# Summing the first head's projection over K-tiles while its modulation is still being loaded, in a two-layer diffusion block

## The chip, the cores and the metric

The kernel runs on one core of a Trainium2 chip. The metric is the device time of one launch in microseconds. The core has five engines that work side by side and meet through semaphores: PE (TensorE, matrix products), DVE (VectorE), ACT (ScalarE), POOL (GpSimd) and SP (SyncE, which here issues most of the DMAs). PEld is the loading of PE's stationary operand.

## What is computed

A latent stream `x` (512 tokens by 1024) and a context stream `ctx` (256 tokens by 1024) pass through two layers; only the latent stream is returned. Each layer is a mixer and a SwiGLU network, each of them behind a norm that is modulated by a conditioning vector:

```
mx = silu(c) @ mod_w[l] + mod_b[l]        # 6 parts of 1024: shift, scale, gate, twice
mc = silu(c_ctx) @ mod_w[l] + mod_b[l]
hx = rms(x, norm_mix_w[l]) * (1 + scx1) + shx1
hc = rms(ctx, norm_mix_w[l]) * (1 + scc1) + shc1
# layer 0: 16 query heads in 4 groups, one key/value head each
#   groups 0, 1: windowed attention with a sink; groups 2, 3: dense attention
p  = h @ ev_w_in                           # queries, keys, values of all groups
q, k = rope(rms(q)), rope(rms(k))          # context tokens without rope
x  = x + gx1 * (attention @ w_out)
x  = x + gx2 * swiglu(rms(x) * (1 + scx2) + shx2)
# ctx likewise; layer 1 is a differential attention of 8 heads with the same frame
```

All inputs are float32. The kernel keeps that precision in its large products by splitting each operand into a rounded part and a remainder and adding three products: high by high, high by low, low by high.

## The kernel before

The 768 tokens are six tiles of 128: tiles 0 to 3 are `x`, tiles 4 and 5 are `ctx`; `CTX_FIRST` is the order 4, 5, 0, 1, 2, 3. The model width of 1024 is eight K-tiles of 128.

**The start.** SP loads the two context tiles, then the modulation weights of parts 0 and 1 (shift and scale of the first norm) in chunks of 256 columns, with the four tiles of `x` among them. `start_mod(n)` makes both parts' chunk `n` through `mod_chunk`: two pieces of 512 KB are loaded (ring `mw` of six, `start_tile`), 16 small products per piece (eight K-tiles' halves, each in two passes) put both streams' results, spread over four strips of partitions, into a PSUM bank (lines 164 to 172), ACT copies them out as `modr` (174), and PE turns the rows into columns with products against a two-column selector `sel2` (179). `add_mod` adds the bias and, for a scale, forms `aff` (227, 231). Chunk `n` gives shift and scale of the K-tiles `2n` and `2n + 1`.

Beside this each token tile is squared and summed on ACT (843), scaled on DVE (844), transposed on PE (848) and copied by ACT into `xT` (849). When all four chunks are written down, a loop over the K-tiles modulates `xT` in place on DVE (854), rounds it to `hT`/`hTc` on ACT (859) and subtracts for the remainder (860), on DVE for the latent tokens and on POOL for the context.

**The first head group.** `weights0(0, ...)` loads four units of projection weights (three DMAs each, 384 KB), rounds them on ACT (309) and subtracts on DVE (310). `in_proj0` then goes over the six token tiles: `project` adds 24 products of 128 by 384 into one bank (405 to 407), ACT copies the sum to the row buffer `qkv` (451, ring of two), and the rotation follows: squares on ACT (379), sums on DVE (381), reciprocal roots on POOL (148, 149), products with the rope tables on DVE (388, 393 to 396), scaling on POOL (454), the split of queries and keys (456 to 461), transposes of both (468, 474), and copies to `qt` and `kT` (470, 475).

**The later groups.** While the attention of group `b` runs, `in_proj0(b + 1)` is interleaved, one tile after each pair of attention steps, with its sums in the single bank `acc0`, and so are the twelve chunks of modulation parts 2 to 4 (`MODS0`). Four chunks of part 5 follow in the first SwiGLU network.

**Order.** The program is written in one order, and a planner that simulates the engines sets the order of the instructions on each engine; `tc.high_priority(n)` ranks the instructions in its block earlier. On the chip each engine then goes through its own list in that order. PSUM has eight banks: `acc0`, `acc1`, `tr0`, `tr1` and two tiles of two banks each in `p_sc`. The weights' landing room `raw_tile` is a ring of two.

## Time and profile before

| | us |
|---|---|
| median of 3 runs | 1822.0 |
| lowest and highest of them | 1819.93, 1823.89 |
| the profiled execution | 1825.45 |
| its span, first to last instruction | 1823.7 |

A view of windows gives, for each stretch, its length and then busy time and number of instructions of PE, PEld, DVE, ACT and POOL, then the clock granted to PE as a share of full speed, the mean busy share of the 16 DMA engines, and GB/s. A timeline row gives start, duration, engine, line, operation, output and inputs, shape and count, and in brackets the idle time before it with what ended it. A row of grouped instructions gives busy time and mean duration in ns of one, then the idle time in front of them. A matmul's duration is longer than the step from its start to the next one's, since matmuls overlap.

### The profile page before, as it was taken

What the parts mean: (1) busy time and instruction counts of PE and PEld (TensorE: products, weight loads), DVE (VectorE), ACT (ScalarE), POOL (GpSimd) and SP (SyncE); (2) the same over time, 40 slices, a digit from 0 to 9 for tenths busy, and PEclk for the clock granted to TensorE, in tenths of its full rate; (3) what the DMA queues carried; (4) which work ended last, traced back from release to release, by engine and by line L of the source; (5) the groups of instructions that cost most, each with busy time, mean ns of one, the idle gap of its engine ahead of it and who ended that gap; (6) DMA issues with size and microseconds to landing.
All of it is one profiled execution on the core that took longest, in us unless ns stands there. A gap on an engine that the chain in (4) does not pass through costs nothing. (4 is left out here: it accounts for less than half of the span.)

```text
span 1823.7 us, 26198 instructions
## 1 busy us (share of the span) xinstructions
PE 1752.0 (96%) x9958; PEld 1458.2 (80%) x9958; DVE 1002.0 (55%) x1703; ACT 825.5 (45%) x1726; POOL 641.8 (35%) x840
## 2 busy tenths in 40 slices
PE   6999999999999999999999899999998999999998
PEld 4877676667888888888888789999986888888886
DVE  4664545443355555545552657777675455655652
ACT  6555555544354444333331656666664532222220
POOL 2764554632053443222220466666643200000000
PEclk8999999999999999999999899999999999999999
DMA  9111322302543334334330311111103233232221
GB/s 314 46 44 55 96 73 99 131 13 76 180 149 117 103 104 140 115 127 126 117 105 3 102 35 59 44 45 44 42 25 104 90 97 102 82 104 93 93 93 47
DMA packets 152478, 165.65 MB, mean 91 GB/s; under 512 B 16480, under 2 KB 139936, under 8 KB 152352
## 3 DMA queue, kind: packets, MB, share of 16 engines
q1 hardware_dynamic: 152000, 163.77, 28.1%
q8 instruction: 78, 1.28, 0.3%
q14 instruction: 48, 0.39, 0.1%
q10 hardware_dynamic: 352, 0.21, 0.0%
HBM read 159.73 MB, written 4.22 MB: 90 GB/s over the span
## 5 line engine op out<-in xcount | busy, mean ns | idle before, releaser
L750 PE MATMUL pg<-hT,wgh 128*128 128x512 f32 (+1 forms) x736 | 244.8, 386 | 2.2 <-ACT hT L293 2.2
L750 PE MATMUL pu<-hT,wuh 128*128 128x512 f32 (+1 forms) x736 | 244.1, 385 | 0.0
L412 DVE TENSOR_TENSOR dps<-dps,g 128x512 f32<-128x512 f32 x200 | 135.7, 697 | 131.3 <-PE dps L801 126.7
L799 PE MATMUL dps<-wdh,hdh 128*128 128x512 f32 x440 | 176.2, 401 | 5.3 <-DVE x L413 3.5
L800 PE MATMUL dps<-wdl,hdh 128*128 128x512 f32 x440 | 174.0, 396 | 0.0
L801 PE MATMUL dps<-wdh,hdl 128*128 128x512 f32 x440 | 166.4, 396 | 0.0
L750 PEld LDWEIGHTS pg<-hT,wgh 128*128 128x128 f32 x736 | 137.2, 189 | 32.7 <-ACT hT L293 2.4
L750 PEld LDWEIGHTS pu<-hT,wuh 128*128 128x128 f32 x736 | 137.1, 189 | 28.5
L750 PE MATMUL pg<-hT,wgl 128*128 128x512 f32 (+1 forms) x368 | 141.9, 386 | 0.0
L750 PE MATMUL pu<-hT,wul 128*128 128x512 f32 (+1 forms) x368 | 141.5, 384 | 0.0
L413 DVE TENSOR_TENSOR x<-x,dps 128x512 f32<-128x512 f32 x200 | 133.3, 683 | 3.3
L405 PE MATMUL inps<-wih,hT 128*128 128x384 f32 x384 | 133.1, 347 | 0.4 <-ACT qkv L451 0.2
L406 PE MATMUL inps<-wil,hT 128*128 128x384 f32 x384 | 130.6, 340 | 0.0
L407 PE MATMUL inps<-wih,hT 128*128 128x384 f32 x384 | 130.6, 340 | 0.0
L198 ACT ACTIVATE modw<-modw,cols 128x256 f32<-128x256 f32 x192 | 81.9, 498 | 69.4 <-DMA modw<-in_mod_w_dram 66.4
L799 PEld LDWEIGHTS dps<-wdh,hdh 128*128 128x128 f32 x440 | 82.7, 188 | 27.6 <-DVE x L413 4.4
L310 DVE TENSOR_TENSOR wul<-wur,wuh 128x1024 fp32r<-128x1024 f32 x44 | 54.6, 1241 | 89.3 <-ACT wuh L309 89.3
L801 PEld LDWEIGHTS dps<-wdh,hdl 128*128 128x128 f32 x440 | 82.6, 188 | 20.2 <-issue 0.4
L750 PE MATMUL pg<-hTc,wgh 128*128 128x256 f32 x352 | 98.3, 283 | 0.5 <-ACT hTc L293 0.2
L750 PE MATMUL pu<-hTc,wuh 128*128 128x256 f32 x352 | 98.2, 282 | 0.0
L800 PEld LDWEIGHTS dps<-wdl,hdh 128*128 128x128 f32 x440 | 82.8, 188 | 17.6
L777 DVE TENSOR_TENSOR pu<-sg,pu 128x768 f32<-128x768 f32 (+1 forms) x44 | 36.5, 829 | 108.3 <-PE pu L750 94.4
(235 smaller groups left out, 4306.3 us busy)
## 6 DMA issues: line engine op xcount, KB each, us to landing
modw<-in_mod_w_dram SPq DMA_DIRECT2D x96, 512.0 KB, 4.0
wgr<-in_ffn_w_in_dram SPq DMA_DIRECT2D x44, 512.0 KB, 3.4
wur<-in_ffn_w_in_dram SPq DMA_DIRECT2D x44, 512.0 KB, 3.4
wdr<-in_ffn_w_out_dram SPq DMA_DIRECT2D x44, 512.0 KB, 3.5
wir<-in_od_w_in_dram SPq DMA_DIRECT2D x96, 128.0 KB, 2.3
x<-in_x_dram SPq DMA_DIRECT2D x8, 512.0 KB, 3.9
wir<-in_ev_w_in_dram SPq DMA_DIRECT2D x16, 256.0 KB, 2.7
wor<-in_ev_w_out_dram SPq DMA_DIRECT2D x8, 512.0 KB, 4.4
```

The lines of the kernel that those rows point to most:

```text
L198: nc.scalar.activation(pr[:, k], w[:, k], AF.Copy, scale=cols[:, kk:kk + 1])
L310: (sub or nc.vector).tensor_sub(lo, raw, f32(hi))
L405: nc.tensor.matmul(ps, hs[0][:, k, :], a, start=k == 0, stop=False)
L406: nc.tensor.matmul(ps, hs[0][:, k, :], b, start=False, stop=False)
L407: nc.tensor.matmul(ps, hs[1][:, k, :], a, start=False, stop=k == KT - 1)
L412: nc.vector.tensor_mul(tmp, ps, g[:, n * 512:(n + 1) * 512])
L413: eng.tensor_add(xt[:, n * 512:(n + 1) * 512], xt[:, n * 512:(n + 1) * 512], tmp)
L750: nc.tensor.matmul(ps[:, s0:s1], a, cols_T(b, s0, s1)[:, k, :], start=k == 0 and q == 0, stop=k == KT - 1 and q == 2)
L777: nc.vector.tensor_mul(pu, sg, pu)
L799: nc.tensor.matmul(ps, hh, a, start=j == 0, stop=False)
L800: nc.tensor.matmul(ps, hh, b, start=False, stop=False)
L801: nc.tensor.matmul(ps, hl, a, start=False, stop=j == nj - 1)
```

## The change

Four parts.

1. The first group's projection is summed by quarters. Chunk `n` of the modulation (`start_mods`) now makes both parts in one PSUM bank with one copy and one set of transposes, ranked ahead of other work by 400; the products' order, its DMAs and its ring (eight in place of six) are in `start_mods` itself. Behind each chunk stands one unit of projection weights (`unit0`). `start_h(n)` modulates, rounds and splits the two K-tiles of that chunk, alternating ACT and DVE for the modulation. Then `project` adds those two K-tiles to all six token tiles, whose six sums stay open in six banks (`acc0`, `acc1`, and four in `p_sc`). `in_proj0(0)` starts from the finished sums (`banks`).
2. Rows become columns by `mod_cols`, in all chunks that `mod_chunk` makes too: a transpose of each block of 128 and a DVE reduction over the four strips, in place of the products with `sel2`.
3. Of each token tile's two copies into `xT`, the second goes to DVE. The first group's weights are split on POOL and land in `raw_tile`, the second group's are split on DVE.
4. The row buffer `qkv` has four places in place of two (`QBUF`). The mask lands in `raw_tile`. The query tiles `qt` of groups 0 and 2 lie in the pool `even` in place of `wp`.

```diff
+QBUF = 4
...
-    mk = start.pool.tile([P, 2, P], F32, name="mk")
+    mk = raw_tile([P, 2, P], "mk")
...
-        pc2 = p_1.tile([P, nb, 2], F32, name="modcol", tag=bank)
+        add_mod(l, part, k0, k1, mod_cols(r, p_1.tile([P, nb, P], F32, name="modcol", tag=bank)), 2)
+
+    def mod_cols(r, ps):
+
+        nb = ps.shape[1]
         for b in range(nb):
-            nc.tensor.matmul(pc2[:, b, :], r[:, b * P:(b + 1) * P], sel2, start=True, stop=True)
-        add_mod(l, part, k0, k1, pc2, 2)
+            nc.tensor.transpose(ps[:, b, :], r[:, b * P:(b + 1) * P], ident)
+        m = small.tile([P, nb, 2], F32, name="mcol", tag=f"mcol{nb}")
+        nc.vector.tensor_reduce(m, ps.rearrange("p b (j r) -> p b r j", r=32)[:, :, 0:2, :], AX.X, ALU.add)
+        return m
...
-    def project(ps, t, ws, c0, c1):
+    def project(ps, t, ws, c0, c1, ks=range(KT)):
...
-        for k in range(KT):
+        for k in ks:
...
         for t in CTX_FIRST:
-            ps = acc_tile("inps", 384, one=0) if b else p_sc.tile([P, 1024], F32, name="inps", tag="sc")[:, :384]
-            project(ps, t, ws, 0, 384)
-            raw = wp.tile([P, 384], F32, name="qkv", tag="qkv", bufs=2)
+            if banks:
+                ps = banks[t]
+            else:
+                ps = acc_tile("inps", 384, one=0)
+                project(ps, t, ws, 0, 384)
+            raw = wp.tile([P, 384], F32, name="qkv", tag="qkv", bufs=QBUF)
...
-        return start.pool.tile(shape, F32, name=name, tag="mw", bufs=6)
-
-    def start_mod(n):
+        return start.pool.tile(shape, F32, name=name, tag="mw", bufs=8)
+
+    def start_mods(n):
+
+        wm = []
         for part in range(2):
-            mod_chunk(0, part, n, raw_tile if n == 3 and part == 0 else start_tile, start.pool, f"acc{part}", p_sc)
+            c0 = part * D + n * 256
+            for pc in range(2):
+                w = start_tile([P, 4, 256], "modw")
+                nc.sync.dma_start(
+                    w, mod_w[0, pc * 4 * P:(pc + 1) * 4 * P, c0:c0 + 256].rearrange("(j p) n -> p j n", p=P))
+                wm.append(w)
+
+        with tc.high_priority(400):
+            ps = tr_tile("mod", [P, 2, 256])
+            for a, w in enumerate(wm):
+                part, pc = divmod(a, 2)
+                for j in range(4):
+                    nc.tensor.matmul(ps[32 * j:32 * j + 32, part, :], s_pad[:, 4 * pc + j, :], w[:, j, :],
+                                     start=pc == 0, stop=pc == 1, tile_position=(0, 32 * j))
+            r = start.pool.tile([P, 512], F32, name="modr", tag="modr", bufs=1)
+            nc.scalar.copy(r, ps.rearrange("p a n -> p (a n)"))
+            m = mod_cols(r, tr_tile("modcol", [P, 4, P]))
+            for part in range(2):
+                add_mod(0, part, 2 * n, 2 * n + 2, m[:, 2 * part:2 * part + 2], 2)
+
+    def start_h(n, segs):
+
+        ks = slice(2 * n, 2 * n + 2)
+        for s0, s1 in segs:
+            i = s0 // SEQ
+            for k in range(2 * n, 2 * n + 2):
+                z = xT[:, k, s0:s1]
+                sc, sh = aff[0][:, 0, k, i:i + 1], modc[0][:, 0, k, i:i + 1]
+                if k % 2:
+                    nc.scalar.activation(z, z, AF.Identity, bias=sh, scale=sc)
+                else:
+                    nc.vector.tensor_scalar(z, z, sc, sh, ALU.mult, ALU.add)
+            hi, lo = (cols_T(j, s0, s1)[:, ks, :] for j in range(2))
+            nc.scalar.copy(hi, xT[:, ks, s0:s1])
+            (nc.gpsimd if i else nc.vector).tensor_sub(lo, xT[:, ks, s0:s1], f32(hi))
...
-    start_mod(0)
-    start_mod(1)
+    start_mods(0)
+    ws = [unit0(0, 0, wp.pool, nc.gpsimd)]
     xs.update({t: load_x(t) for t in CTX_FIRST[2:]})
...
-            nc.scalar.copy(xT[:, 4 * g:4 * g + 4, t * P:(t + 1) * P], pt)
-    start_mod(2)
-    start_mod(3)
-    for k in range(KT):
...
+            (nc.vector.tensor_copy if g else nc.scalar.copy)(xT[:, 4 * g:4 * g + 4, t * P:(t + 1) * P], pt)
+
+    banks = {t: acc_tile("inps", 384) for t in CTX_FIRST[:2]}
+    for t in (0, 2):
+        two = p_sc.tile([P, 2, 512], F32, name="inps", tag="sc")
+        banks.update({t + a: two[:, a, :384] for a in range(2)})
+    for n in range(4):
+        if n:
+            start_mods(n)
+            ws.append(unit0(0, n, wp.pool, nc.gpsimd))
+        start_h(n, ((SEQ, TOK), (0, SEQ)) if n else ((SEQ, TOK), (0, SEQ // 2), (SEQ // 2, SEQ)))
+        for t in CTX_FIRST:
+            project(banks[t], t, ws, 0, 384, range(2 * n, 2 * n + 2))
...
-    proj = in_proj0(0, ws, tabs, wp.pool, even.pool, wp.pool)
+    proj = in_proj0(0, ws, tabs, wp.pool, even.pool, even.pool, banks)
...
-            ws = weights0(b + 1, wp.pool, nc.gpsimd)
-            proj = in_proj0(b + 1, ws, tabs, wp.pool, (even if b % 2 else odd).pool, (wp if b % 2 else odd).pool)
+            ws = [unit0(b + 1, u, wp.pool, nc.gpsimd if b else nc.vector) for u in range(4)]
+            proj = in_proj0(b + 1, ws, tabs, wp.pool, (even if b % 2 else odd).pool, (even if b % 2 else odd).pool)
```

`unit0(b, u, ...)` is the body of the loop in `weights0`, for one unit.

27 lines of the change are left out of this document (7 added, 20 removed).

## The prediction

> **What bounds the kernel now.** I read the page's busy table first, then its slices, then the windows of the first 85 us and the timeline of TensorE (PE) there, because every edit but one lies in that stretch.
>
> ```profile
> PE 1752.0 (96%) x9958; PEld 1458.2 (80%) x9958; DVE 1002.0 (55%) x1703; ACT 825.5 (45%) x1726; POOL 641.8 (35%) x840
> PE   6999999999999999999999899999998999999998
> DMA  9111322302543334334330311111103233232221
> ```
>
> PE is busy nearly everywhere, the DMA engines only in the first slice of 45.6 us. So the kernel is a DMA-bound head, followed by a PE-bound rest. A microsecond of PE work moved out of the rest into the head is worth up to a microsecond at the end, provided PE then finds other work. The windows show the head in bytes (last column, GB/s), clock (PEclk) and PE time.
>
> ```profile
> 0.00:10.00 10.00, 1.75 (x13) 0.61 (x17) 1.14 (x3) 5.45 (x9) 2.38 (x10) 1.00 0.82 284
> 10.00:20.00 10.00, 9.76 (x65) 5.50 (x57) 1.95 (x5) 5.17 (x10) 0.84 (x3) 1.00 1.06 402
> 20.00:30.00 10.00, 7.04 (x72) 5.10 (x72) 5.72 (x14) 8.53 (x19) 3.66 (x7) 1.00 1.07 376
> 30.00:40.00 10.00, 7.26 (x57) 3.70 (x57) 6.85 (x14) 4.58 (x9) 1.86 (x1) 0.61 1.04 325
> 40.00:50.00 10.00, 10.00 (x45) 10.00 (x46) 9.93 (x18) 4.24 (x8) 7.00 (x2) 0.70 0.27 75
> ```
>
> That is 2.84, 6.86, 10.62 and 13.87 MB in by 10, 20, 30 and 40 us, and then the stream stops. The first projection starts only there:
>
> ```profile
> 40.78 0.67 PE L405 MATMUL inps<-wih,hTc 128*128 128x384 f32 x1
> 41.25 0.52 PE L406 MATMUL inps<-wil,hTc 128*128 128x384 f32 x1
> 41.57 0.52 PE L407 MATMUL inps<-wih,hTc 128*128 128x384 f32 x1
> ...
> 45.80 0.49 PE L405 MATMUL inps<-wih,hTc 128*128 128x384 f32 x1
> 46.13 0.34 PE L406 MATMUL inps<-wil,hTc 128*128 128x384 f32 x1
> 46.30 0.34 PE L407 MATMUL inps<-wih,hTc 128*128 128x384 f32 x1
> ...
> 53.45 0.48 ACT L451 COPY qkv<-inps 128x384 f32<-128x384 f32 x1 [1.90 <-PE inps L407]
> ...
> 72.26 0.33 PE L407 MATMUL inps<-wih,hT 128*128 128x384 f32 x1
> ```
>
> From start to start a projection matmul takes 0.32 us up to 45.8 and 0.173 us after it. The 144 of them (6 tiles, 8 K-tiles, 3 each) run from 40.8 to 72.4; ScalarE (ACT) takes out the first finished sum at 53.45.
>
> **The change: the projection by quarters.** It cuts the 144 matmuls into four groups of 36, each needing only its quarter of the modulation, and holds six sums open in six banks. What a quarter waits for: x (6 tiles, 0.52 MB each), its modulation weights (4 pieces of 0.52 MB) and its projection weights (0.39 MB). These bytes are the same as before, in another order: x now comes behind four pieces of modulation and one of the projection.
>
> ```profile
> 28.01 1.07 ACT L849 COPY xT<-npt 128x512 f32<-128x512 f32 x2
> ...
> 38.05 1.93 PE L171 MATMUL mod<-modw,s_pad 128*32 128x256 f32 x16
> 39.91 1.01 PE L179 MATMUL modcol<-cst,modr 128*128 128x2 f32 x4
> ...
> 42.25 5.17 POOL L860 TENSOR_TENSOR hTc<-xT,hTc 128x512 fp32r<-128x512 f32 x1 [7.81 <-ACT hTc L859]
> ...
> 46.37 1.07 DVE L231 SCALAR_TENSOR_TENSOR aff<-modc,cols 128x4 f32<-128x4 f32 x1
> ...
> 51.58 1.35 DVE L860 TENSOR_TENSOR hT<-xT,hT 128x512 fp32r<-128x512 f32 x1 [0.34 <-ACT hT L859]
> ```
>
> Before, x is all transposed at 29.1 us. With one modulation group less ahead of it (1 MB at 376 to 402 GB/s, some 2.6 us) and half of the evictions moved from ACT to VectorE (DVE), whose windows up to 30 us have room, I estimate 24 us: the first quarter can run over all six tiles from there. The last modulation needs all of x, 16 pieces and three projection units, with 0.4 MB of small inputs 13.1 MB: 10.62 at 30 us and 2.5 more at 325 GB/s give 37.6 us. In the kernel before its scale is done only at 47.4, since the last column matmuls stood behind projection matmuls, and the last operand at 52.9. Ranked first, they follow their weights directly:
>
> ```profile
> 144.59 0.65 PE L553 MATMUL av<-PT,vv 128*64 128x256 f32 x4
> ...
> 145.82 1.07 PE L171 MATMUL mod<-modw,s_pad 128*32 128x256 f32 x16
> 146.83 0.77 PE L543 MATMUL ppt<-cst,Pt 128*128 128x128 f32 x5
> ...
> 148.57 0.56 PE L179 MATMUL modcol<-cst,modr 128*128 128x2 f32 x4
> 148.99 0.64 PE L543 MATMUL ppt<-cst,Pt 128*128 128x128 f32 x4
> 149.56 0.65 PE L553 MATMUL av<-PT,vv 128*64 128x256 f32 x4
> ```
>
> At the full clock 16 modulation matmuls take 1.01 us, four column matmuls 0.42 and four transposes 0.57 from start to start. The last chain is then 1.0 for the last matmuls, some 0.6 for the copy (half of the x2 row above), 0.57 for four transposes, and for the new DVE reduction, which this trace does not show, 0.2 to 0.5 us: between a tiny DVE operation and the 128x320 reduction quoted below. I take 0.3, as it sums only 32 values per partition. With the two small additions and the hand-overs I put it at 3.7 us: 41.3. Modulating, rounding and subtracting a quarter of two K-tiles costs about 4 us more (the x2 row of ACT, 1.07, and the L860 row of DVE, 1.35, are two of three steps), and the context part's subtraction on GpSimd (POOL) ran 5.17 us here, beside a DVE busy 9.93 of 10. So the last quarter's operands are whole at 45 to 47, and by data alone the projection could end at 47 + 24 x 0.173, some 51 us.
>
> PE itself is later. From 24 us it has 132 of the 144 matmuls left (the context tiles' first 12 may go earlier), 22.8 us at 0.173; three modulation groups of 32 matmuls, 6.1 us; their 12 transposes, 1.7. That is 30.6 us: 54.6, and I take **55 us**. The bounds are 50 (data, everything earlier hidden) and 60 (30.6 us begun at 26, with one stretch of 16 matmuls at 0.32, 2.4 us, and a us of waits). Before, the same point is 72.4 less what PE did in between of other work: four tiles' query and key transposes and the last two column groups, together about 2.2 us, so 70.2. **Head start: 15 us** (10 to 20).
>
> **What of it carries.** After 55, PE lives on head 1's projection (25 us) until head 0's rotations have come through. Those are longest on POOL:
>
> ```profile
> L149 POOL TENSOR_TENSOR rs_q<-rs_q,neghalf 128x5 f32<-128x5 f32 x12 | 14.5, 1204 | 0.3
> L454 POOL TENSOR_TENSOR qy<-qy,rs_q 128x320 f32<-128x320 f32 x12 | 8.7, 722 | 0.4
> L381 DVE TENSOR_REDUCE qss<-sq 128x5 f32<-128x320 f32 x12 | 5.8, 479 | 3.5 <-ACT sq L379 3.5
> L461 POOL TENSOR_TENSOR kd<-qy,kd 128x128 fp32r<-128x128 f32 x11 | 5.6, 512 | 2.6 <-ACT es L527 1.7 <-POOL vv L452 0.8
> L452 POOL COPY vv<-qkv 128x64 f32<-128x64 f32 x12 | 4.5, 376 | 2.1 <-ACT qkv L451 2.0
> L148 POOL TENSOR_SCALAR rs_q<-qss 128x5 f32<-128x5 f32 x12 | 3.4, 287 | 8.5 <-DVE qss L381 5.9 <-DVE nm L519 1.8 <-DVE rc L530 0.2
> ```
>
> One tile costs POOL 1.20 + 0.72 + 0.51 + 0.38 + 0.29 = 3.1 us, six 18.6. Six sums now become ready within some 6 us instead of over 19, so this chain turns from hidden to nearly bare: from about 50 to 69, against head 1's projection from 55 to 80. Its cover holds, thinly. Four row buffers instead of two let PE run ahead of the rotation, and head 1's weights can be loaded and split early, since each quarter of head 0's frees its unit. Their subtraction moves from POOL to DVE, four of them, while head 0's moves to POOL, beside the DMA stream, at no cost. I take 4 us of lost PE time (0 to 10). From 110 us on, PE is full again:
>
> ```profile
> 75.00:80.00 5.00, 3.17 (x13) 1.84 (x12) 4.37 (x15) 4.02 (x12) 4.83 (x7) 1.00 0.23 65
> 80.00:85.00 5.00, 4.98 (x24) 4.98 (x25) 2.86 (x14) 3.91 (x14) 3.65 (x9) 0.66 0.29 80
> ...
> 110.00:120.00 10.00, 9.87 (x69) 8.88 (x68) 6.48 (x17) 7.26 (x19) 6.41 (x10) 1.00 0.01 2
> ```
>
> **The columns of later modulations.** Sixteen chunks after the start exchange four column matmuls (0.42 us) for two transposes (0.29): 0.13 us each, 2 us in all on a full PE, with one DVE reduction more in each; the bank is held by one DVE read as before. **The other homes** (mask, query tiles, ring of eight) move no work; I cost them nothing. If an address newly shared makes a wait, it costs about one eviction, 0.5 us per head, and a gain from them is excluded as no transfer starts earlier but those in the head.
>
> **Sum.** 15 - 4 + 2 = **13 us**: the profiled execution's 1825.45 (span 1823.7) becomes 1812.5. That execution is 3.45 above the median of the three runs, 1822.0, which the same saving makes **1809.0**.
>
> **The rivals.** *Rotation-bound (0.18).* If POOL and DVE, not PE, set when head 0's attention can start, only their advance carries: the first sum is ready some 4 to 8 us earlier than its 53.45. With 2 for the columns the gain is about 7: 1815. For it: POOL is busy 4.83 of 5 at 75 to 80, and PE idles there. Against it: those 5 us also carry weight splits that now come earlier, on DVE.
>
> *The stall goes too (0.12).* The 1.83 us of idle PE at 75 to 80 and the low clock after it (0.66, about 1.7 us lost) vanish, nothing is lost, and the data bound is met: 19 + 2 = 21 less, 1801.
>
> *No overlap (0.08).* Engines run in a planned order. If the planner puts the early quarters behind the last modulation, PE waits at its head for the last DMA, and 144 matmuls follow it: what is left is the shorter last chain and the columns, 2 us: 1820.
>
> *Cold quarters (0.12), the slower one.*
>
> ```profile
> 30.00:35.00 5.00, 2.81 (x24) 1.70 (x28) 4.99 (x9) 2.27 (x5) 1.86 (x1) 0.73 1.10 373
> 35.00:40.00 5.00, 4.45 (x37) 1.99 (x29) 1.86 (x6) 2.31 (x4) 0.00 (x0) 0.50 0.98 276
> 40.00:45.00 5.00, 5.00 (x17) 5.00 (x18) 5.00 (x12) 4.13 (x7) 2.75 (x1) 0.50 0.26 71
> ```
>
> After a window with PE busy 2.81 of 5 the clock granted falls to half, and it takes 5 us of solid matmuls to come back. If each quarter is met by a wait, all 132 matmuls run at 0.32 instead of 0.173 (19.4 us more) and six groups of 16 modulation matmuls at 1.86 instead of 1.01 (5.1 more). The projection then ends near 53 + 24.5 = 77, 7 us later than before's 70.2; less 2 for the columns that is 5 us lost, 1827. It turns into a loss once some 105 of the 132 run cold. Against it: a quarter brings 36 x 0.173 + 2.0 + 0.6 = 8.8 us of PE work, while its 2.5 MB take 6.3 to 7.7 us to come, so PE has no gap to cool in; and the windows of 10 to 30 us had full clock with less work.
>
> The Trainium skill ("TensorE: Matmul & The Clock Gate", section "HAM oscillation — how this bites in real kernels") speaks against just this form: a loop over K-tiles with a DMA wait between them loses the clock at every K-tile, and it advises doing all K-tiles before waiting. By that rule the result would be this rival's; the trace agrees that gaps cost the clock, but not that this load leaves the gaps.
>
> **Chances.** Forecast 0.50, with its own range 1804 to 1815; rivals as given. A measurement of this kernel tells some 0.2% (3.6 us) from no change. Faster: 0.50 + 0.18 + 0.12 = 0.80; the same: 0.08; slower: 0.12. The range 1800 to 1820 reaches from the stall's case to no overlap and leaves out the slow case and thin tails.
>
> **What would show it.** Right: L405 matmuls from about 24 us at 0.173, clock near 1 from 20 to 50, the last of head 0's at 50 to 60, scores starting near 65, PE without gaps from there, the ends of later phases all some 13 us earlier. Wrong: no projection matmul before 38 us (no overlap); 0.32 spacing through the quarters (cold); projection over at 55 but PE idle for 5 us or more between 55 and 90 behind POOL or DVE (rotation-bound); or gains in the head lost again after 360 us, which none of my cases has.

## The result, and the profile after

The changed kernel took 1839.91 us (median of 4 runs, 1839.26 to 1841.77) beside 1822.95 for the kernel before: a ratio of 1.0091, interval 1.0076 to 1.0106, some 17 us slower. The forecast was 1809.0, in a range of 1800 to 1820. The profiled execution took 1841.77 us, its span 1840.0.

The busy row and PE's slices on the page of the changed kernel:

```profile
PE 1747.4 (95%) x9910; PEld 1454.4 (79%) x9910; DVE 1008.7 (55%) x1719; ACT 825.4 (45%) x1722; POOL 641.6 (35%) x840
PE   7899999798999999999999889999998899999998
```

PE does 4.6 us less in a span 16.3 us longer. A slice is 46 us; new 7s and 8s stand in the second slice (46 to 92 us), the eighth (322 to 368) and the tenth (414 to 460), and much later two single 8s, in the 24th and the 32nd. The windows of its head (columns as in the prediction: length, then PE, PEld, DVE, ACT, POOL, the clock, the DMA share, GB/s):

```profile
20.00:30.00 10.00, 8.42 (x47) 7.65 (x48) 6.13 (x12) 7.51 (x15) 4.63 (x8) 0.83 1.11 356
30.00:40.00 10.00, 8.53 (x94) 6.21 (x92) 3.35 (x10) 5.40 (x10) 2.78 (x2) 1.00 0.92 278
40.00:50.00 10.00, 10.00 (x77) 7.90 (x77) 7.01 (x10) 5.00 (x7) 5.83 (x4) 1.00 0.29 88
50.00:60.00 10.00, 7.75 (x44) 7.09 (x43) 4.92 (x12) 4.55 (x6) 1.30 (x1) 0.98 0.54 151
60.00:70.00 10.00, 10.00 (x51) 10.00 (x50) 6.65 (x15) 7.27 (x15) 6.29 (x13) 0.85 0.28 75
70.00:80.00 10.00, 7.81 (x41) 7.07 (x39) 7.79 (x16) 3.40 (x9) 9.37 (x13) 0.83 0.15 40
80.00:90.00 10.00, 8.10 (x45) 7.77 (x45) 6.81 (x20) 7.09 (x20) 8.10 (x14) 0.83 0.00 0
```

The quarters do overlap the loads, at a clock of 0.98 to 1.00 from 30 to 60 us. But the stream stays under 300 GB/s from 30 us on, PE waits between 55 and 60, and between 70 and 90 it is busy 15.9 of 20 us, while GpSimd is busy 17.5. The timeline of PE at the last quarter:

```profile
46.07 0.64 PE L853 MATMUL mod<-modw,s_pad 128*32 128x256 f32 x8
47.54 0.64 PE L853 MATMUL mod<-modw,s_pad 128*32 128x256 f32 x8
52.21 0.60 PE L183 MATMUL modcol<-cst,modr 128*128 128x128 f32 x4
58.20 0.44 PE L411 MATMUL inps<-wih,hTc 128*128 128x384 f32 x1 [2.25 <-ACT hTc L874]
...
66.22 0.34 PE L413 MATMUL inps<-wih,hT 128*128 128x384 f32 x1
66.40 0.34 PE L411 MATMUL inps<-wih,hTc 128*128 128x384 f32 x1
```

The last product of the first group starts at 66.22, the second group's follow: 66.6, not 55. And then the stage of the fourth group, group 3. Windows of the two kernels there, before and then after, and below them two rows of PE's waits after (line, what it waited for, us in total, times, longest; 300 to 450 us):

```profile
320.00:360.00 40.00, 38.15 (x217) 24.80 (x215) 19.31 (x32) 23.62 (x43) 30.22 (x21) 1.00 0.44 145
360.00:400.00 40.00, 37.10 (x194) 26.77 (x196) 14.93 (x29) 15.97 (x33) 9.53 (x11) 1.00 0.04 14
```

```profile
320.00:360.00 40.00, 34.02 (x196) 19.86 (x194) 18.77 (x29) 25.42 (x44) 33.11 (x23) 1.00 0.43 139
360.00:400.00 40.00, 32.91 (x154) 23.36 (x154) 11.92 (x24) 14.00 (x29) 7.32 (x9) 0.87 0.06 20
```

```profile
PE ops L725 <- POOL wol L316: 5.3, 2, 4.7
PE ops L724 <- DVE x L419: 3.1, 2, 1.6
```

PE waits for `wol`, the remainders of the output-projection weights, for which it waits nowhere in these 150 us before. It is also granted a clock of 0.87 in place of 1.00 from 360 to 400 us. The timeline of ACT shows why the weights are late. Before, the first of these weights is rounded (`woh`) right behind the last query tile of group 3:

```profile
312.38 0.58 ACT L470 CAST qt<-qpt 128x512 fp32r<-128x512 f32 x1 [0.63 <-PE qpt L468]
313.13 2.01 ACT L309 CAST woh<-wor 128x1024 fp32r<-128x1024 f32 x2
...
324.32 0.38 ACT L556 COPY o<-av 128x256 f32<-128x256 f32 x1
```

After, it stands behind the last attention copy of group 2, 12 us later, though its weights had been asked for at 289 us:

```profile
314.65 0.59 ACT L477 CAST qt<-qpt 128x512 fp32r<-128x512 f32 x1 [0.35 <-PE qpt L475]
325.33 0.38 ACT L563 COPY o<-av 128x256 f32<-128x256 f32 x1 [0.77 <-PE av L560]
325.60 2.00 ACT L315 CAST woh<-wor 128x1024 fp32r<-128x1024 f32 x2
```

**Where the time went.** Marks that every trace has: the start of the last ACT copy `o<-av` of a group of layer 0 (the end of its attention), the first `qpt` transpose of layer 1 and the first `pg` product behind it (between them lies layer 1's attention). Group 3's stage runs from group 2's mark to its own. All in us; the ratio to the kernel before is from the timed runs, the rest is from each profile.

| kernel | ratio (95%) | group 0 ends | group 2 ends | group 3's stage | layer 1's attention | span |
|---|---|---|---|---|---|---|
| before | 1 | 167.7 | 324.3 | 99.0 | 379.3 | 1823.7 |
| after | 1.0091 (1.0076–1.0106) | 179.8 | 325.3 | **115.8** | 376.8 | 1840.0 |
| b_homes | 1.0115 (1.0102–1.0128) | 166.8 | 321.6 | **115.2** | 381.8 | 1842.8 |
| b_homes0 | 1.0278 (1.0264–1.0292) | 167.0 | 326.4 | **111.7** | 409.9 | 1868.7 |
| b_w4 | 1.0191 (1.0174–1.0207) | 166.9 | 326.4 | 99.1 | 408.6 | 1854.3 |
| two | 1.0051 (1.0039–1.0064) | 181.4 | 327.9 | 99.7 | 379.0 | 1829.0 |
| two_q2 | 1.0043 (1.0029–1.0058) | 168.8 | 323.1 | 99.0 | 386.1 | 1830.7 |
| two_by_tile | 1.0065 (1.0051–1.0079) | 176.5 | 325.6 | 99.3 | 380.7 | 1825.0 |
| two_sel2 | 1.0021 (1.0008–1.0033) | 181.6 | 326.1 | 99.0 | 380.2 | 1825.4 |
| homes_back | 1.0002 (0.9992–1.0013) | 168.7 | 323.3 | 99.0 | 376.7 | 1817.9 |
| hb_split | 1.0021 (1.0012–1.0031) | 172.5 | 326.5 | 99.0 | 382.4 | 1827.0 |
| hb_rot | 1.0008 (0.9999–1.0017) | 167.1 | 321.9 | 99.0 | 381.4 | 1823.1 |
| sel2 | 1.0027 (1.0016–1.0037) | 167.7 | 324.3 | 99.0 | 380.5 | 1825.4 |
| sel2_rot | 1.0008 (0.9998–1.0018) | 167.7 | 322.8 | 99.0 | 377.5 | 1820.0 |
| sel2_split | 1.0172 (1.0159–1.0185) | 169.1 | 324.1 | 99.0 | **409.1** | 1854.4 |
| split_pool | 1.0113 (1.0098–1.0128) | 176.2 | 326.5 | **112.4** | 383.5 | 1841.7 |
| b_cols | 1.0017 (1.0006–1.0028) | 170.0 | 324.9 | 99.6 | 382.6 | 1826.1 |
| early | 1.0060 (1.0043–1.0077) | 175.2 | 329.8 | 99.0 | 385.6 | 1834.3 |
| b_hi2 | 0.9993 (0.9982–1.0005) | 164.6 | 319.4 | 99.8 | 382.2 | 1824.2 |

The changed kernel against the one before: 1.0 us late at the end of group 2, 16.8 more in group 3's stage, 2.5 given back in layer 1's attention, the rest within about 1: 16.3 of span. So two questions: what holds the output weights (16.8), and why nothing of a forecast 13 us is left at the end of group 2. The profile of b_hi was taken at a mean granted clock of 0.844 and is not in the table; the same kernel was profiled again as b_hi2.

### The profile page after: what moved, and what is told of

It is laid out like the page before. It is cut to its first block, busy times and chain, and to the rows that moved or that the text cites. A ratio compares the mean times of both kernels' runs of the same rounds, so it can differ in the third digit from the quotient of the medians.

```text
span 1840.0 us, 26146 instructions
## 1 busy us (share of the span) xinstructions
PE 1747.4 (95%) x9910; PEld 1454.4 (79%) x9910; DVE 1008.7 (55%) x1719; ACT 825.4 (45%) x1722; POOL 641.6 (35%) x840
## 5 line engine op out<-in xcount | busy, mean ns | idle before, releaser
L540 POOL TENSOR_SCALAR Pt<-Pt,rc 128x256 f32<-128x256 f32 (+3 forms) x96 | 70.9, 751 | 79.3 <-DVE rc L537 60.8
```

Source lines behind the costliest of these rows:

```text
L540: nc.gpsimd.tensor_scalar(p[:, :n], p[:, :n], rc[:, hh:hh + 1], 1.0, ALU.mult, ALU.mult)
```

## The experiments: the output weights

**b_homes**: the kernel before, with the new home of the query tiles of groups 0 and 2 only.

```diff
-    proj = in_proj0(0, ws, tabs, wp.pool, even.pool, wp.pool)
+    proj = in_proj0(0, ws, tabs, wp.pool, even.pool, even.pool)
...
-            proj = in_proj0(b + 1, ws, tabs, wp.pool, (even if b % 2 else odd).pool, (wp if b % 2 else odd).pool)
+            proj = in_proj0(b + 1, ws, tabs, wp.pool, (even if b % 2 else odd).pool, (even if b % 2 else odd).pool)
```

> The kernel before, with one thing of the change only: the query tiles of groups 0 and 2 in the pool `even` instead of `wp`. Theory (homes): the first output-projection weights then lie on the six query tiles of group 2, so their rounding waits for the end of group 2's attention; the head stays as before, and the end comes 8 to 15 us after the kernel before, with the first woh copy about 325 us instead of 313, and PE losing 8 to 12 us of busy time between 320 and 400 us. Rival (the loss comes from the head's own delay, passed on): no difference beyond 2 us, since the head is untouched.

Measured 1844.5 us, 1.0115: all of the loss, and more, from these two lines (some 21 us, where 8 to 15 were expected). The stage takes 115.2 us, the first `woh` copy comes at 321.84, right behind the last attention copy of group 2 (321.57), and PE loses 8.7 us of busy time between 320 and 400. The rival falls.

**homes_back**: the changed kernel with those two lines as before; the smaller rings make it fit.

```diff
-QBUF = 4
+QBUF = 2
...
-        m = small.tile([P, nb, 2], F32, name="mcol", tag=f"mcol{nb}")
+        m = small.tile([P, nb, 2], F32, name="mcol", tag=f"mcol{nb}", bufs=2)
...
-        return start.pool.tile(shape, F32, name=name, tag="mw", bufs=8)
+        return start.pool.tile(shape, F32, name=name, tag="mw", bufs=6)
...
-    proj = in_proj0(0, ws, tabs, wp.pool, even.pool, even.pool, banks)
+    proj = in_proj0(0, ws, tabs, wp.pool, even.pool, wp.pool, banks)
```

The call for the later groups ends in `(wp if b % 2 else odd).pool` again.

> The changed kernel with its part 4 largely undone: query tiles of groups 0 and 2 back in `wp`, the row buffer back to two places, the modulation ring back to six (all three are needed for it to fit). Theory (homes): the first woh copy is back at or before 313 us and the loss after 320 us goes: 1823 to 1829, 10 to 17 us under the changed kernel. Rival (the loss comes from the head): the end stays within 3 us of the changed kernel's 1840, or later by up to 5 because two row buffers hold the rotation up.

Measured 1823.47, 1.0002 (0.9992 to 1.0013): the first `woh` copy is back at 311.39 us, the stage at 99.0, and the loss is gone, by 16 us. But nothing is gained over the kernel before either.

Why does a home matter? In the compiled program the weights' pool `w0` begins at byte 163,808 of each partition. The pool `even` ended at 162,112; in the changed kernel, with 12 KB of query tiles, it ends at 174,784. So `w0` now overlaps `even`. It could be that only query tiles still in use hold the weights up, or that a pool's memory is handed over as a whole.

The compiled order, laid beside the trace, already speaks for the second. In the changed kernel the last read of a query tile of group 2 is a score product at 307.61 us, within the first row below, 18 us before the weights are rounded. What reads `even` last is the product with the values `vv` in the second row, which ends group 2's attention. The values lie at bytes 160,960 to 162,496, where `w0` does not reach, but in the same pool.

```profile
307.05 0.94 PE L516 MATMUL sc<-kT,qt 128*128 128x256 f32 x4
...
324.63 0.65 PE L560 MATMUL av<-PT,vv 128*64 128x256 f32 x4
```

**b_homes0**: the kernel before, with the query tiles of group 0 alone in `even`, and smaller rings to make room. Where `w0` overlaps `even` there are then only tiles that nobody reads after 168 us. **b_w4** is its control: the smaller rings alone.

```diff
-WBUF = 5
+WBUF = 4
...
-    proj = in_proj0(0, ws, tabs, wp.pool, even.pool, wp.pool)
+    proj = in_proj0(0, ws, tabs, wp.pool, even.pool, even.pool)
...
-            kd = wp.tile([P, 2, 2, HD], F32R, name="kd", tag="kd", bufs=2)
+            kd = wp.tile([P, 2, 2, HD], F32R, name="kd", tag="kd", bufs=1)
```

> The kernel before, with the query tiles of group 0 alone in `even` (those of group 2 stay in `wp`), and, to make room, four places for the projection weights in place of five and one for the key tiles kd. The output-projection weights then lie on query tiles of group 0 only, which nobody reads after 170 us. Theory (the pool is handed over as a whole, whoever used the bytes): the first woh copy still stands behind the end of group 2's attention, near 325 us, and the end is 14 to 24 us after the kernel before, 1837 to 1847. Rival (only a query tile still in use holds the weights up): the end within 4 us of before's 1823, plus at most 3 us for the smaller rings.

> The kernel before with four places for the projection weights and one for the key tiles kd, the control of b_homes0. Theory (whole pools are handed over): the fourth group's stage, from the end of group 2's attention to the end of group 3's, takes 99 to 100 us as before, where b_homes0 has 111.7, while the attention of layer 1 takes some 410 us as in b_homes0, since the same ring of weights reorders it: 1850 to 1858 in all. Rival (the smaller rings make b_homes0's loss): 110 us or more in the fourth group's stage, 1868 to 1876 in all.

The timeline of ACT in b_homes0:

```profile
314.46 0.58 ACT L470 CAST qt<-qpt 128x512 fp32r<-128x512 f32 x1 [0.62 <-PE qpt L468]
326.39 0.37 ACT L556 COPY o<-av 128x256 f32<-128x256 f32 x1 [0.77 <-PE av L553]
326.67 2.00 ACT L309 CAST woh<-wor 128x1024 fp32r<-128x1024 f32 x2
```

The weights still wait for group 2's end, though no byte they lie on is in use. The stage takes 111.7 us, in the control 99.1. Both kernels lose another 29 to 31 us in layer 1's attention; that comes with the rings, not the home, and is why b_homes0 missed its range. Shown: the weights wait until the last reader in the overlapped pool is done, whichever bytes it reads. The wait is in the order that the planner gave to ACT's list: in the compiled program the rounding itself waits for nothing but its weights' DMA, and stands behind that copy.

**two**: the changed kernel, all of its edits kept, with the weights in two pools: 52 KB that share no byte with `even`, and 12 KB (the remainders of the sixth to eighth K-tile) that do. `LoRing` takes five remainders from the one and three from the other. The weights of the first SwiGLU network use the same two pools.

```diff
-            wp = Pool("w0", "right")
+            wp, wp2 = Pool("w0", "right"), Pool("w0b", "right")
+            two = (wp.pool, LoRing(wp.pool, wp2.pool))
...
-            oproj = OutProj(0, out_units(wp.pool, ev_w_out), o_t, xs, opa.pool)
+            oproj = OutProj(0, out_units(two, ev_w_out), o_t, xs, opa.pool)
```

> The changed kernel, all of its four parts kept, with one thing mended: the 64 KB of output-projection weights lie in two pools, 52 KB that share no byte with `even` and 12 KB (the remainders of the sixth to eighth K-tile) that do. Theory (memory is handed over pool by pool: any tile of the pool w0 waits for everything in a pool that it overlaps): the first woh copy comes near 313 us again, PE's busy time between 320 and 400 us is back at 74 to 75 us, and the time is 14 to 21 us under the changed kernel: 1819 to 1826. Rival (the wider head ring, the four row buffers and the moved splits carry the loss): within 4 us of 1840.

The timeline of ACT in two:

```profile
316.14 0.59 ACT L486 CAST qt<-qpt 128x512 fp32r<-128x512 f32 x1 [0.35 <-PE qpt L484]
316.62 2.00 ACT L324 CAST woh<-wor 128x1024 fp32r<-128x1024 f32 x2
```

The weights follow the last query tile again, the stage takes 99.7, PE is busy 38.65 and 36.16 us in the two windows: the mechanism holds. The time, 1830.8, is 9 us better than the changed kernel and above my range, since group 2 ends 2.6 us later and layer 1's attention takes 2.2 more.

## The experiments: where the head start went

**split_pool**, **hb_split** and **sel2_split** put the second group's weight splits back on GpSimd, in the changed kernel, in homes_back and in sel2 (below).

```diff
-            ws = [unit0(b + 1, u, wp.pool, nc.gpsimd if b else nc.vector) for u in range(4)]
+            ws = [unit0(b + 1, u, wp.pool, nc.gpsimd) for u in range(4)]
```

> The changed kernel with the second group's weights split on GpSimd as before, not on VectorE. Theory (VectorE's queue): the reduction of the last modulation no longer stands behind a split that waits for its own weights, so it comes about 3 us earlier (52 instead of 55.5), the last quarter with it, and the first group's projection ends near 61 to 63 instead of 66; at the end 0 to 4 us are left of it, since GpSimd then carries the splits beside the rotations: 1836 to 1840. Rival (GpSimd, already over 4.5 of 5 us busy at 70 to 85, is what bounds the rotations): the attention starts later by 3 us or more and the end is 2 to 6 us later, 1842 to 1846.

> homes_back with the second group's weights split on GpSimd as before. The end of group 2's attention within 1.5 us of homes_back's 323.3 and the total within 4 us of it either way (theory: the split's place is worth nothing by then). Rival (three us of earlier last operands are carried through): 320 us there, and 3 us less at the end.

> As sel2, with the second group's weights split on GpSimd as before. Theory (a split waiting for its weights stands ahead of the last modulation's reduction on VectorE, 3 us): the last operands come 3 us earlier; but the rotations on GpSimd set the start of the attention, and four splits of 1.8 us more lie there, so the end is the same within 2 us, or up to 4 us later. Rival (the last operands set it): 2 to 3 us earlier than sel2.

The timeline of DVE, the changed kernel first, then split_pool:

```profile
54.62 0.96 DVE L316 TENSOR_TENSOR wil<-wir,wih 128x768 fp32r<-128x768 f32 x1 [3.77 <-ACT wih L315]
55.49 0.18 DVE L185 TENSOR_REDUCE mcol<-modcol 128x8 f32<-128x32 f32 x1
```

```profile
52.44 0.19 DVE L185 TENSOR_REDUCE mcol<-modcol 128x8 f32<-128x32 f32 x1 [1.99 <-PE modcol L183]
```

A moved split waits for its own weights and holds the last modulation's reduction behind it on DVE: 3.05 us, as expected. In split_pool the projection ends at 64.3 us, not at 61 to 63, and group 0 ends 3.7 us earlier, but by the end of group 2 that is gone (326.5 against 325.3). In hb_split and sel2_split there is nothing of it (group 2 ends at 326.5 against homes_back's 323.3, which misses the 1.5 us expected, and at 324.1 against sel2's 324.3). Of the totals 1827.1 (hb_split) lies within its 4 us. 1843.2 (split_pool) lies in the rival's range, though group 0's attention doesn't end later, as the rival says. 1854.5 (sel2_split) is far out: there the place of four splits in the head costs 26 us, all of it in layer 1's attention, 409.1 us against sel2's 380.5.

**early**: homes_back, with the modulation of chunks 1 to 3 computed from chunk 0's weights.

```diff
+    first_wm = []
+
     def start_mods(n):
 
-        wm = []
-        for part in range(2):
+        wm = first_wm
+        for part in range(0 if n else 2):
```

> The kernel with the homes of before (homes_back), but the modulation of the second to fourth chunk is computed from the first chunk's weights, so 6.3 MB less are loaded in the head (the output is then not the reference's). The last modulation is ready some 15 us earlier. Theory (late operands swallowed the head start): the first group's projection ends at 50 to 55 us, as forecast, where homes_back has 67, and the end of group 2's attention, 323.3 us in homes_back, comes 8 to 14 us earlier, the end as well. Rival (the rotations and the first attention steps on GpSimd, VectorE and ScalarE pace the stage from 55 to 120 us, so PE time gained ahead of them is lost in it): the projection ends at 50 to 55 all the same, PE idles more from 55 to 95 us, and group 2's attention ends 0 to 5 us earlier.

Both theories fail. With 6.3 MB less to load the last modulation is copied out no earlier, at 51.53 us against homes_back's 50.61, the 144th projection product ends at 70.1 us (67.7), and group 2 ends 6.5 us later. The timelines of ACT, homes_back and then early, and early's windows:

```profile
50.61 0.59 ACT L856 COPY modr<-mod 128x512 f32<-128x512 f32 x1 [0.38 <-PE mod L853]
```

```profile
51.53 0.59 ACT L858 COPY modr<-mod 128x512 f32<-128x512 f32 x1 [2.20 <-PE mod L855]
```

```profile
20.00:40.00 20.00, 12.10 (x88) 9.70 (x88) 13.71 (x18) 11.35 (x19) 10.19 (x11) 0.91 0.32 88
40.00:55.00 15.00, 14.33 (x109) 10.60 (x110) 6.75 (x17) 8.54 (x14) 2.36 (x2) 0.77 0.21 55
```

The DMA engines are mostly idle there (88 and 55 GB/s), so it is not the bytes that make the modulation late in this kernel. In the changed kernel, too, the stream has run dry before the last modulation products at 47.54: 140 GB/s from 42 to 44 us, 8 from 44 to 46. Each quarter passes through PE, ACT and DVE several times, and on each its steps stand in one list with the other quarters' products, weights and transposes. What a fast chain through these lists would give, early does not show.

**b_hi** and **b_hi2** measure what a head start on PE is worth: the kernel before, with 96 of the first projection's 144 matmuls left out.

```diff
-            nc.tensor.matmul(ps, hs[0][:, k, :], a, start=k == 0, stop=False)
+            nc.tensor.matmul(ps, hs[0][:, k, :], a, start=k == 0, stop=hi and k == KT - 1)
+            if hi:
+                continue
...
-                project(ps, t, ws, 0, 384)
+                project(ps, t, ws, 0, 384, b == 0)
```

> The kernel before, where the first group's projection adds only the product high by high: 96 of its 144 matmuls are left out (the output is less exact). 39 of the 96 lie ahead of the 45.8 us where the step falls from 0.32 to 0.173, so the projection takes some 20 us less of PE (two thirds of 72.4 - 40.8 = 31.6 us). It measures what a head start on PE is worth, by itself. Theory (the rotations and first attention steps on GpSimd, VectorE and ScalarE pace the stage to 120 us): group 2's attention ends only 3 to 9 us earlier than before's 324.3. Rival (a microsecond of PE in the head is worth one at the end, as forecast): 14 to 20 us earlier. Beyond that point the difference is kept within 1 us up to layer 1.

> The same kernel as b_hi (the kernel before with 96 of the first projection's 144 matmuls left out), for a profile at the full clock. b_hi's total was that of the kernel before, ratio 1.0004. Theory (GpSimd, VectorE and ScalarE pace the stage to 120 us): the first group's attention ends within 5 us of before's 167.7 and group 2's within 6 us of 324.3, GpSimd over 4 of 5 us busy from 55 to 90 us, and PE idle there for most of what was left out. Rival (the gain is there and layer 1's order takes it back): group 2's attention ends 14 us or more earlier, and the attention of layer 1 takes 390 us or more in place of 379.

Some 20 us of PE work less give 1.0004 and 0.9993: nothing. In b_hi2 group 0 ends 3.0 us earlier and group 2 4.9 us earlier, which the theory allowed and the rival did not. At layer 1's first query transpose 2.6 of the 4.9 are left, and its attention takes 2.9 more. Windows from 55 to 95 us, before and then b_hi2, and a row of b_hi2's waits (45 to 180 us):

```profile
55.00:75.00 20.00, 20.00 (x128) 19.68 (x127) 13.55 (x28) 11.56 (x28) 16.49 (x24) 1.00 0.06 18
75.00:95.00 20.00, 17.93 (x96) 15.92 (x96) 10.45 (x38) 12.35 (x39) 17.87 (x30) 0.91 0.22 60
```

```profile
55.00:75.00 20.00, 14.38 (x66) 11.97 (x65) 14.25 (x29) 12.81 (x30) 18.76 (x28) 0.80 0.19 53
75.00:95.00 20.00, 19.55 (x119) 18.86 (x119) 15.54 (x45) 11.98 (x40) 17.27 (x29) 0.95 0.09 24
```

```profile
PE inps L408 <- POOL wil L310: 7.8, 4, 2.8
```

Before, PE is busy 20 of 20 us, but with work that it needn't do then. GpSimd is busy 16.5 and 17.9 of 20, with the rotations of group 0 and the weight splits of group 1. Take PE's work away, and GpSimd goes to 18.8 while PE waits for its splits (2.7 us at 49 us, 2.3 between 55 and 75, 2.8 after 115).

Where did the 20 us go? An estimate from the windows: from 40 to 115 us PE is idle 7.6 us more than before, less than the expected "most of what was left out". Nearly as much goes to the clock: it is granted 0.56 in place of 0.80 from 40 to 55 us, 0.80 in place of 1.00 from 55 to 75, and 0.95 in place of 0.91 from 75 to 95, together some 7 us of full clock. That leaves about the 4.9 us seen. So PE's fullness was not what bound this stage; that GpSimd alone sets its pace is not shown, and the runs don't separate the waits from the clock. The Trainium skill ("Perfetto Trace Analysis", section "Identifying the Most-Contended Engine") says that PE's matmul busy share is no good measure of how close PE is to its roofline, because pipelined instructions look smaller in the trace. These windows give another reason for the same caution: work done ahead of its need.

**hb_rot** and **sel2_rot** take the value copies and key subtractions of the first group off GpSimd, in homes_back and in sel2.

```diff
-            nc.gpsimd.tensor_copy(vv[:, t, :], raw[:, 320:384])
+            (nc.scalar.copy if banks else nc.gpsimd.tensor_copy)(vv[:, t, :], raw[:, 320:384])
...
-            nc.gpsimd.tensor_sub(kd[:, 1], kb, f32(kd[:, 0]))
+            (nc.vector if banks else nc.gpsimd).tensor_sub(kd[:, 1], kb, f32(kd[:, 0]))
```

> homes_back with the first group's value copies on ScalarE and its key subtractions on VectorE. Theory (GpSimd is one of three engines that pace the first rotations): group 2's attention ends 0.5 to 2 us earlier than in homes_back, as in the version of it with the selector products (322.8 against 324.3), and the total is 1820 to 1823. Rival: no difference there, and the total is within the changes that the order of layer 1 makes, 1820 to 1828.

> As sel2, with two of GpSimd's five rotation steps taken from it for the first group: the copy of the values goes to ScalarE, the subtraction for the keys to VectorE (0.9 of 3.1 us for each tile). Theory (GpSimd paces the first group's rotations once six sums are ready together): the last query tiles of group 0 are copied 2 to 5 us earlier (92 us in homes_back), and the end comes 1 to 4 us earlier than sel2. Rival (VectorE, over 4 us busy of 5 there, paces them just as much): within 1 us of sel2, or later.

Some 5 us less on GpSimd, and group 2 ends 1.4 and 1.5 us earlier. The sign that the theory named for it shows in one of the two only: the last query tile of group 0 is copied 1.7 us earlier in hb_rot, 0.3 later in sel2_rot. The totals follow layer 1: sel2_rot takes 1824.9 against sel2's 1828.6, hb_rot 1824.9 against 1823.5, layer 1 giving (377.5 for 380.5) and taking (381.4 for 376.8) more than that.

**two_q2** is two with `QBUF = 2`. **two_by_tile** is two with the products written down behind the loop over the chunks, token tile by token tile, so that the early tiles rank first:

```diff
-        for t in CTX_FIRST:
-            project(banks[t], t, ws, 0, 384, range(2 * n, 2 * n + 2))
+    for t in CTX_FIRST:
+        project(banks[t], t, ws, 0, 384)
```

> The kernel in two pools, with two row buffers qkv in place of four. Theory (with four buffers the second group's projection runs out early, and the attention of group 0 then has nothing beside it: PE busy 6.46 of 10 and clock 0.75 after it between 115 and 135 us): PE is full there, its busy time between 95 and 180 us is back from 78.1 to 81 or more, and the end comes 3 to 6 us earlier than in two pools. Rival (four buffers are what let PE run ahead while the rotations of group 0 hold the attention up): more PE idle between 70 and 95 us, and the end 2 to 6 us later.

> The kernel in two pools, with the first group's projection written down tile by tile (all eight K-tiles of token tile 4, then of tile 5, and so on), where the change has it quarter by quarter over all six tiles. Theory (the rotation is bare because six sums come ready within 5 us): sums become ready one after another, PE's idle time and low clock between 70 and 90 us shrink by 2 to 5 us, and the end comes 1 to 5 us earlier than in two pools. Rival (GpSimd's 3 us for each tile set the pace whichever sum comes first): within 1 us, or up to 3 us later since early quarters run later.

In two_q2 group 2 ends 4.8 us earlier and PE is busy 82.0 of 85 us from 95 to 180, not 78.1. So the four row buffers cost 4.8 us. They let PE start more projection products before 110 us (288, in two_q2 262), which group 0's attention then lacks beside it. The rival's sign is there too: from 55 to 95 us PE is busy 1.7 us less than in two. The total does not show the gain (1832.0), for layer 1's attention takes 7.1 more. In two_by_tile PE's busy time from 55 to 95 us rises from 32.5 to 35.0 and group 2 ends 2.3 us earlier, but the total, 1832.8, cannot be told from two's 1830.8.

## The experiments: the columns

**b_cols** is the kernel before with `mod_cols` in all its chunks; **two_sel2** and **sel2** are two and homes_back with the selector products back in the 16 later chunks (the edit below).

```diff
-        add_mod(l, part, k0, k1, mod_cols(r, p_1.tile([P, nb, P], F32, name="modcol", tag=bank)), 2)
+        pc2 = p_1.tile([P, nb, 2], F32, name="modcol", tag=bank)
+        for b in range(nb):
+            nc.tensor.matmul(pc2[:, b, :], r[:, b * P:(b + 1) * P], sel2, start=True, stop=True)
+        add_mod(l, part, k0, k1, pc2, 2)
```

> The kernel before, with transposes and a VectorE reduction in place of the selector products in all its modulation chunks, and nothing else. The forecast's term: 2 us less (16 chunks of 0.13 us). Rival: VectorE's extra reduction waits behind its other work and holds the bank longer, so nothing is gained or 1 to 3 us lost.

> The kernel in two pools, with the products against the two-column selector back in the 16 later modulation chunks (the head keeps its transposes). Forecast's term: 2 us slower than the kernel in two pools (16 chunks of 0.13 us). Rival (the reduction on VectorE, and the copy to SBUF it adds to the chain, costs at least what PE saves): the same within 1.5 us, or up to 3 us faster.

> The kernel with the homes of before (homes_back) with the products against the two-column selector back in the 16 later modulation chunks; the head keeps its transposes and quarters. Theory (the new columns cost 3 to 4 us in two pools and would here): 2 to 4 us under homes_back, that is 1819 to 1822 and ratio 0.997 to 1.000 to the kernel before. Rival (the forecast's term): 1825 to 1827.

Per chunk the step is as forecast. Grouped rows of PE from 100 to 320 us (12 chunks), before and then after:

```profile
L179 PE MATMUL modcol<-cst,modr 128*128 128x2 f32 x48 | 6.7, 244 | 0.0
```

```profile
L183 PE MATMUL modcol<-cst,modr 128*128 128x128 f32 x24 | 4.7, 277 | 0.0
```

2 us of PE in 12 chunks. At the end of group 2 the runs don't agree. sel2, with the selector back, is 1.0 later than homes_back. b_cols, with the new columns, is 2.3 us late at the end of group 0 and 0.5 late here. two_sel2 is the other way: with the selector back it is 1.8 earlier than two. The totals, b_cols 3 us slower than before, two_sel2 4 faster than two and sel2 5 slower than homes_back, are in part layer 1's. So the forecast's 2 us are not shown at the end: the effect is too small to be told from what follows.

## Layer 1's attention, which nobody touched

Its program is the same in all kernels, its time lies between 376.7 and 409.9 us. Go through the lists of PE, DVE, ACT and GpSimd there, by operation and tile. They are the same in before, sel2_rot and two_sel2 (379.3, 377.5 and 380.2 us), and one other order is shared by b_homes, b_hi2, b_cols and split_pool (381.8 to 383.5): one order, one time, within 3 us. In sel2_split 1135 of some 2330 places in PE's list write another tile than in sel2, and in b_homes0 and b_w4 1485 another than before: those three take 409 to 410 us. Windows of the stretch, before and then b_homes0:

```profile
1058.00:1437.00 379.00, 357.04 (x2328) 331.44 (x2328) 250.65 (x436) 227.31 (x564) 216.28 (x331) 0.98 0.16 49
```

```profile
1072.00:1482.00 410.00, 372.60 (x2334) 347.02 (x2333) 244.16 (x436) 231.90 (x565) 222.72 (x332) 0.93 0.15 46
```

About half of the 31 us is idle time of PE (37.4 us against 22.0), the other half the same products at a clock of 0.93 in place of 0.98. The edits stand far ahead, so the planner must carry a small shift in the head through to the end; against before its order there is worth up to 2.5 us for the better and 30.6 for the worse. So the totals of kernels that differ by less than some 9 us say little about their heads, and I judge the heads by the marks up to group 3. No version here beats both kernels: homes_back, hb_rot and sel2_rot beat the changed one and equal the one before.

## Why the prediction was wrong

**The other homes: the step that failed.** I costed them at nothing, or 0.5 us for an address newly shared. The address was shared, and the wait was for a whole pool to fall free: 16.8 us in group 3's stage, and 16.2 by the two lines alone. I had looked at the wait per eviction, not at who hands the memory over. "Gains in the head lost again after 360 us, which none of my cases has" is where it showed, save that there was no gain to lose.

**The head start of 15 us.** By my own reckoning it was 3.6 (70.2 less 66.6). The steps: x is transposed at 29.9 us, not 24, and the last scale is done at 56.1, not 41.3:

```profile
29.31 0.59 ACT L892 COPY xT<-npt 128x512 f32<-128x512 f32 x1 [0.89 <-PE npt L891]
...
55.98 0.16 DVE L237 SCALAR_TENSOR_TENSOR aff<-modc,cols 128x4 f32<-128x4 f32 x1
...
57.53 0.62 ACT L874 CAST hTc<-xT 128x512 fp32r<-128x512 f32 x1
```

I had added up bytes and one bare chain. The chain was sized well piece by piece (the reduction takes 0.18 us for an assumed 0.3), but its pieces stand in lists: the last transposes (52.21) come 3.4 us after the copy that they need, behind projection products, and the reduction 2.7 us after them, behind the moved split, which I had placed "beside the DMA stream, at no cost". But how much of the 11.6 us between 55 and 66.6 is the chain's? Windows of the changed kernel from the last transposed copy of x on (PE's wait lies between the last two rows):

```profile
29.90:40.00 10.10, 8.63 (x95) 6.31 (x93) 3.42 (x10) 5.50 (x10) 2.78 (x2) 1.00 0.92 279
40.00:55.95 15.95, 15.95 (x111) 13.49 (x110) 9.16 (x16) 6.68 (x9) 5.83 (x4) 1.00 0.35 104
58.20:66.56 8.36, 8.36 (x37) 8.06 (x38) 6.26 (x13) 5.60 (x10) 4.29 (x9) 0.80 0.49 134
```

PE is full from 40 to 55.95 us with the first three quarters and the last modulation, so the late chain costs it only the wait of 2.25 us, an earlier one of 1.5 us in the first row, and some 1.7 us of full clock in the last row (8.36 us at 0.80). The largest term is the start: 5.9 us because x came late, of an estimate that I had made from bytes and from room on DVE. Part of the reason stands on ACT, where the squares of x's last two tiles (at 22.38 and 25.35 us) share one list with the modulation and rounding of the first quarter; how much that costs is open.

**What the rotations got of it: less than nothing.** I reckoned with sums that are ready "within some 6 us" and with rotations from about 50 to 69. All six sums close in the last quarter, so the first one, which the kernel before takes out at 53.45, now comes at 61.98, and the last query tile of group 0 is copied at 95.11 where it was 88.44. Timelines of ACT, after and then before:

```profile
61.98 0.47 ACT L458 COPY qkv<-inps 128x384 f32<-128x384 f32 x1
...
95.11 0.59 ACT L477 CAST qt<-qpt 128x512 fp32r<-128x512 f32 x1 [1.68 <-PE qpt L475]
```

```profile
88.44 0.59 ACT L470 CAST qt<-qpt 128x512 fp32r<-128x512 f32 x1
```

So the projection ends earlier by 3.6 us and what depends on it comes later by 6.7: the sums are kept open for all six tiles until the last modulation.

**"PE then finds other work": the deeper miss.** I took PE as the bound of the stage behind the head because it was busy there, and 4 us as the loss. b_hi2 shows that 20 us of PE work less are worth 4.9 at the end of group 2, so 15 us of head start would not have carried 11 to the end. The rival "rotation-bound" came nearest to this with 0.18 and 7 us. But its premise, a first sum 4 to 8 us earlier, failed as well (8.5 later), and which engine sets the rotations' pace is not shown: in the changed kernel PE's waits from 70 to 90 us are 2.6 us for ACT, 0.9 for GpSimd and 0.4 for DVE. Even with the homes mended, homes_back is 1.0 us ahead at that mark.

**Right:** the first quarter's products start at 22.05 us on the context tiles (at 27.99 on x); the column step is 0.17 us cheaper per chunk on PE, for 0.13 forecast; and the quarters did not run cold. The Trainium skill ("TensorE: Matmul & The Clock Gate", section "HAM oscillation — how this bites in real kernels") has a loop over K-tiles, each with less work than the wait for the next one's data, lose the clock at every K-tile. By the windows the clock is 0.83 from 20 to 30 us and 0.98 to 1.00 from 30 to 60, and falls once more, to 0.85 from 60 to 70, behind the wait of 2.25 us at 58: two partial losses in four quarters, not one in each.

## What to carry to other kernels

A buffer that changes its pool can delay a much later stage: look up which later pool now lies on its pool, and which tile of that pool is read last. Sums that are all kept open finish together: ask when the first one is ready, not only the last. An engine that is full because it works ahead is no bound: look for the engine that the others wait for, and take work away from the full one to see whether anything moves. With an order planned over the whole program, judge an edit by marks close behind it, since an untouched stage can move by more than the edit is worth.

## What the runs showed that I had not expected

With two thirds of the first projection's products left out, PE's granted clock fell from 1.00 to 0.80 between 55 and 75 us, while GpSimd was busy 18.8 of the 20 us. So leaving work out cost PE clock as well. And layer 1's attention spans 376.7 to 409.9 us with the order of its instructions. In the three kernels with 409 to 410 us the clock granted there is 0.93 to 0.94, beside 0.98 before, although over the whole execution it is 0.974 to 0.979, beside 0.985.
